# ConvFFN up-projection: the contraction in two halves of the rows, each half in banks of its own

## The chip, the cores and the metric

The kernel runs on one core of one Trainium2 chip. Its time is what the device took from start to end of one execution, in microseconds (us). Two executions of the kernel before took 2832.43 and 2834.16 us, median 2833.3. The core has five engines that run side by side, each through its own list of instructions in order: TensorE (PE; its weight loads stand apart as PEld), VectorE (DVE), ScalarE (ACT), GpSimd (POOL) and SyncE (SP, which starts the DMA transfers). An instruction that has to wait for another engine waits on a semaphore, and everything behind it on its own engine waits with it. TensorE multiplies a moving operand by a stationary one that a weight load has put in place; it sums over the 128 partitions (rows) of both and adds the result up in a bank of PSUM, of which there are eight.

## The reference

One step of a streaming encoder with four layers, over 512 prompt rows and 64 sample rows of width 1024. Each layer is a token mixer (attention, a convolution module or a spatial-gating MLP) followed by a channel mixer, and it is the latter that the change touches:

```python
def _conv_ffn(h, state, w_up, w_dw, b_dw, w_down):
    up = h @ w_up                                   # 1024 -> 2 * 2816
    xp = jnp.concatenate([state, up], axis=1)
    g, u = jnp.split(_dwconv(xp, w_dw, b_dw), 2, axis=-1)   # causal, width 3
    return (jax.nn.gelu(g) * u) @ w_down, xp[:, -(FFN_CONV_WIDTH - 1):]
```

RMSNorm stands before and after each mixer, and the results are added to the residual.

## The kernel before, in words

Activations lie transposed, channels on partitions and the 576 rows (512 and 64) along the free axis, which is cut into a half of 256 and a half of 320 columns. Every number is split into a high and a low part in fp32r, so that a product takes three matmuls for each 128 of the contraction: high by high, high by low, low by high (`mm3`, lines 278 to 280). With eight blocks of 128 in the width of 1024, a product of one half is 24 matmuls into one bank.

The channel mixer (`ffn`, called once a layer) runs over 22 pairs. Pair p holds 128 columns of the gate (q = 0) and the same 128 of the other branch (q = 1). `wload` fetches a weight tile, ScalarE casts its high part in two pieces of 512 columns (line 247) and VectorE takes the difference as the low part (line 250). Four buffers hold high parts, so the casts of pair p + 2 need the buffers of pair p. For each half (hf = 0 with 256 columns, hf = 1 with 320), `finish` runs product q = 0, then product q = 1, and then `evacuate`: VectorE multiplies a product by the norm's row factors and puts it from its bank into a buffer (`ub`, lines 791 and 793). After both halves come GpSimd's copies of the last columns (`fo`), then for each q a convolution of width 3 as one ScalarE activation (line 802) and two VectorE operations (803, 804), a GELU on ScalarE (806), the product of the two branches (808, 809), and the split of the result into `ah` (ScalarE cast, line 812) and `al` (VectorE, 813).

After pairs 3, 7, 11 and 15 a block of the down-projection runs (`block`, 192 matmuls into banks that VectorE adds to `o_y`, line 528), after pair 21 the last two. Pairs 0 and 1 of each layer are begun while the layer's first half ends (`between`), by an order written out by hand; all else is put in order by a scheduler at build time, which places every engine's instructions by a model of the durations, and the chip then follows that order.

Accumulators of all products share a pool of six banks (tag `mm`), two more banks serve small sums. A bank is taken when the first matmul of a product is written down (`bank`), and a later product that gets the same bank waits until the instructions that read it are done. The tag `t` of six work buffers holds the convolution's results.

The same halves of the rows, 0 to 63 and 64 to 127, are used by attention's scores (line 1108): 64 rows of contraction, one head in each half.

Of the kernel before, what the change touches and what calls it, by code (L numbers as in the profile page):

```python
# [12 lines left out]
ALU = mybir.AluOpType  # L13
# [4 lines left out]
P = 128  # L18
# [3 lines left out]
HALF = ((0, 256), (256, 320))  # L22
# [110 lines left out]
def encoder_step_kernel(  # L133
# [12 lines left out]
    V, S, G, T = nc.vector, nc.scalar, nc.gpsimd, nc.tensor  # L146
# [18 lines left out]
    def mm_tile(name):  # L165
        return mmp.tile([P, 512], F32, tag="mm", name=name)
# [13 lines left out]
    def w_tile(name, shape, dt=F32):  # L180
        return wp.tile(shape, dt, tag="t", name=name)
# [78 lines left out]
    def lo_eng(n):  # L260
        return V if n >= POOLW else None
# [10 lines left out]
    def mm3(ps, items, start=0, stop=None):  # L272
# [3 lines left out]
        for i in range(start, n if stop is None else stop):  # L276
# [2 lines left out]
            T.matmul(ps, lh, rl, start=False, stop=False)  # L279
            T.matmul(ps, ll, rh, start=False, stop=(i == n - 1))  # L280

    def bank(name, m=P, n=512):

        made = []

        def get():
            if not made:
                made.append(mm_tile(name)[:m, :n])
            return made[0]

        return get
# [24 lines left out]
    def finish(parts):  # L316
        for part in parts:
            if part:
                for product in part[0]:
                    product.all()  # L320
                part[1]()


    def rsqrt_steps(name, ps, n, scale, eps):
# [57 lines left out]
    def half(t, hf):  # L382
        a, n = HALF[hf]
        return t[:, a : a + n]
# [124 lines left out]
    class Output:  # L509
# [15 lines left out]
        def evacuate(self, m, hf, ps, first, last, square=True):  # L525
            ys = half(self.y[m], hf)
            if not first:
                V.tensor_tensor(ys, ps, ys, ALU.add)  # L528
            elif self.bias is not None:
                S.activation(ys, ps, AF.Identity, bias=self.bias[:, m : m + 1])  # L530
            else:
                S.copy(ys, ps)
            if last and square:
                self.sq[hf].add(ys)
                if self.final:
                    S.activation(ys, ys, AF.Copy, scale=gain(self.i, self.s, m))
# [221 lines left out]
    def ffn(i):  # L758
# [9 lines left out]
        def pair(p):  # L768
            n = f"f{i}_{p}"
            ws = []  # L770
            for q in range(2):
                ws.append(wload(f"{n}_w{q}", w_up, 0, KD, q * FF + p * P, P, lo_eng(p)))
                yield
            ub = []

            def begin():
                for q in range(2):
                    c = q * NF + p
                    ub.append(up.tile([P, 580], F32, tag="ub", name=f"{n}_ub{q}"))
                    G.memset(ub[q][:, 0:2], 0.0)  # L780
                    G.tensor_copy(ub[q][:, 514:516], ct[:, 4:6, c])

            for hf in range(2):
                ps = [bank(f"{n}_p{hf}{q}", n=HALF[hf][1]) for q in range(2)]

                def evacuate(hf=hf, ps=ps):
                    if hf == 0:
                        begin()
                    for q in range(2):
                        b = 2 + hf * 256  # L790
                        V.tensor_tensor(ub[q][:, b : b + 256], ps[q]()[:, :256], h.R[:, hf * 256 : hf * 256 + 256], ALU.mult)  # L791
                        if hf == 1:
                            V.tensor_tensor(ub[q][:, 516:580], ps[q]()[:, 256:320], h.R[:, 512:576], ALU.mult)

                yield [Product(ps[q], h.products(ws[q], hf)) for q in range(2)], evacuate
            cv = [None, None]
            for q in range(2):
                c = q * NF + p
                G.tensor_copy(fo[:, 0, :, c], ub[q][:, 512:514])  # L799
                G.tensor_copy(fo[:, 1, :, c], ub[q][:, 578:580])  # L800
                y = w_tile(f"{n}_c{q}", [P, 578])
                S.activation(y, ub[q][:, 2:580], AF.Identity, bias=ct[:, 3, c : c + 1], scale=ct[:, 2, c : c + 1])  # L802
                V.scalar_tensor_tensor(y, ub[q][:, 1:579], ct[:, 1, c : c + 1], y, ALU.mult, ALU.add)  # L803
                V.scalar_tensor_tensor(y, ub[q][:, 0:578], ct[:, 0, c : c + 1], y, ALU.mult, ALU.add)  # L804
                cv[q] = y
            S.activation(cv[0], cv[0], AF.Gelu_apprx_tanh)
            am = w_tile(f"{n}_a", [P, NT])
            V.tensor_tensor(am[:, 0:512], cv[0][:, 0:512], cv[1][:, 0:512], ALU.mult)
            V.tensor_tensor(am[:, 512:576], cv[0][:, 514:578], cv[1][:, 514:578], ALU.mult)  # L809
            a_hi[p] = b_tile(f"{n}_ah", [P, NT], F32R)  # L810
            a_lo[p] = b_tile(f"{n}_al", [P, NT], F32R)
            S.copy(a_hi[p], am)  # L812
            V.tensor_tensor(a_lo[p], am, a_hi[p].bitcast(F32), ALU.subtract)
# [13 lines left out]
        h = Norm(i, 2)  # L827
        begun = [pair(p) for p in range(2)]
        yield h, begun
        out = Output(i, 3)  # L830
        b = 0
        for p in range(NF):
            finish(begun[p] if p < 2 else pair(p))
            if b < len(FBLK) - 2 and p == sum(FBLK[b]) - 1 + FLAG:
                block(b)
                b += 1
# [1042 lines left out]
```

## Time and profile before

| | |
|---|---|
| median of two runs | 2833.3 us |
| profiled execution: time, span of its instructions | 2833.9 us, 2832.1 us |
| TensorE busy; its weight loads | 2758.0 us (97%); 2637.5 us (93%) |
| VectorE, ScalarE, GpSimd busy | 1857.0 us (66%), 1137.5 us (40%), 383.4 us (14%) |
| mean granted TensorE clock | 0.986 of full speed |
| up-projection matmuls (`f_p` on lines 278 to 280) | 8064, 13% of the chain on each line |
| down-projection matmuls (`o_p`, the same lines) | 9% of the chain on each line |

A busy share is an average over the whole span. Matmuls are pipelined: one lasts longer than the distance to the next, so the distance between starts tells the pace. The chain is followed back from the last instruction, at each step to what released it or to the instruction before it on its engine. An idle time in square brackets is that of the engine just before the instruction, with the one that ended it.

### The profile page before, as it was taken

The numbers are of one execution on the slowest core, as the hardware profiler recorded it, in microseconds if no ns is written. First come the engines' busy times: TensorE is split into PE (matmuls) and PEld (weight loads), VectorE is DVE, ScalarE is ACT, GpSimd is POOL, SyncE is SP. The second block draws the span as 40 slices with busy tenths as digits, with TensorE's granted clock in tenths as the row PEclk, the third lists the DMA queues.
The fourth block names the chain that finished last, engine by engine and source line by source line (L and its number), as shares of the span: only waits on it lengthen the run. The fifth ranks groups of instructions, "written<-read, shape, count | busy, mean of one in ns | idle before, by whom it ended". The sixth has DMA issues, their size and how long they took to land.

```text
span 2832.1 us, 52926 instructions
## 1 busy us (share of the span) xinstructions
PE 2758.0 (97%) x20841; PEld 2637.5 (93%) x20841; DVE 1857.0 (66%) x4194; ACT 1137.5 (40%) x2392; POOL 383.4 (14%) x937
## 2 busy tenths in 40 slices
PE   8999999999878999999999999999999999999998
PEld 7889999998666899999999999999999978999998
DVE  5668666656867576667657567666666676766674
ACT  4655433334123553334434324432333664533343
POOL 3122111110000021111002011211110121211111
PEclk9999999999888999999999999999999999999999
DMA  5322322322332232222233222322222421322221
GB/s 165 87 51 72 93 87 75 90 70 66 95 97 54 68 98 77 89 81 89 68 91 101 75 71 61 90 83 83 82 83 79 105 49 47 93 88 82 83 83 58
DMA packets 359183, 230.72 MB, mean 81 GB/s; under 512 B 44595, under 2 KB 349463, under 8 KB 358807
## 3 DMA queue, kind: packets, MB, share of 16 engines
q1 hardware_dynamic: 358934, 227.34, 28.0%
q8 instruction: 164, 2.69, 0.4%
q14 instruction: 85, 0.69, 0.1%
HBM read 212.87 MB, written 7.45 MB: 78 GB/s over the span
## 4 chain that ended last, share of the span: by engine, by line
PE 89%; DVE 4%; DMA 3%; SPq 2%; ACT 1%; issue 1%; POOL 0%; POOLq 0%; ACTq 0%; DVEq 0%
PE f_p L278 13%; PE f_p L279 13%; PE f_p L280 13%; PE o_p L278 9%; PE o_p L280 9%; PE o_p L279 9%; DVE v_cv L1380 2%; PE m_u_p L278 1%; PE m_u_p L280 1%; PE m_u_p L279 1%; PE m_vp L278 1%; PE m_vp L279 1%; PE m_vp L280 1%; PE t_o L1169 1%; PE t_qp L278 1%; PE t_sp L1108 1%
## 5 line engine op out<-in xcount | busy, mean ns | idle before, releaser
L278 PE MATMUL f_p<-n_hi,f_w_h 128*128 128x320 f32 (+1 forms) x2688 | 799.1, 297 | 0.0
L280 PE MATMUL f_p<-n_hi,f_w_l 128*128 128x320 f32 (+1 forms) x2688 | 797.3, 297 | 0.0
L279 PE MATMUL f_p<-n_lo,f_w_h 128*128 128x320 f32 (+1 forms) x2688 | 797.3, 297 | 0.0
L278 PEld LDWEIGHTS f_p<-n_hi,f_w_h 128*128 128x128 f32 x2688 | 510.1, 190 | 4.5 <-issue 4.1
L279 PEld LDWEIGHTS f_p<-n_lo,f_w_h 128*128 128x128 f32 x2688 | 510.1, 190 | 0.0
L280 PEld LDWEIGHTS f_p<-n_hi,f_w_l 128*128 128x128 f32 x2688 | 510.1, 190 | 0.0
L278 PE MATMUL o_p<-f_ah,f_d_h 128*128 128x256 f32 (+1 forms) x1408 | 418.8, 298 | 2.4 <-ACT f_d_h L247 2.4
L279 PE MATMUL o_p<-f_al,f_d_h 128*128 128x256 f32 (+1 forms) x1408 | 417.6, 297 | 0.0
L280 PE MATMUL o_p<-f_ah,f_d_l 128*128 128x256 f32 (+1 forms) x1408 | 417.2, 297 | 0.0
L247 ACT CAST f_w_h<-f_w_f 128x512 fp32r<-128x512 f32 x352 | 200.7, 618 | 494.9 <-issue 237.8
L528 DVE TENSOR_TENSOR o_y<-o_p,o_y 128x256 f32<-128x256 f32 (+1 forms) x432 | 195.1, 455 | 261.9 <-PE o_p L280 260.5
L791 DVE TENSOR_TENSOR f_ub<-f_p,n_R 128x256 f32<-128x256 f32 x352 | 148.1, 422 | 286.9 <-PE f_p L280 282.2
L278 PEld LDWEIGHTS o_p<-f_ah,f_d_h 128*128 128x128 f32 x1408 | 268.0, 190 | 4.2 <-ACT f_d_h L247 2.6
L280 PEld LDWEIGHTS o_p<-f_ah,f_d_l 128*128 128x128 f32 x1408 | 267.9, 190 | 0.4 <-issue 0.2
L279 PEld LDWEIGHTS o_p<-f_al,f_d_h 128*128 128x128 f32 x1408 | 268.0, 190 | 0.2 <-issue 0.2
L250 DVE TENSOR_TENSOR f_w_l<-f_w_f,f_w_h 128x512 fp32r<-128x512 f32 x352 | 228.9, 688 | 20.3 <-ACT f_w_h L247 18.2
L247 ACT CAST f_d_h<-f_d_f 128x512 fp32r<-128x512 f32 x176 | 101.3, 619 | 231.9 <-PE f_p L279 174.3
L803 DVE SCALAR_TENSOR_TENSOR f_c<-f_ub,f_ct,f_c 128x578 f32<-128x578 f32 x176 | 143.8, 820 | 38.2 <-ACT f_c L802 38.1
L799 POOL COPY f_fo<-f_ub 128x2 f32<-128x2 f32 x176 | 46.7, 266 | 888.0 <-DVE f_ub L791 881.1
L802 ACT ACTIVATE f_c<-f_ub,f_ct 128x578 f32<-128x578 f32 x176 | 150.8, 863 | 1.4 <-POOL f_fo L799 0.7
L812 ACT CAST f_ah<-f_a 128x576 fp32r<-128x576 f32 x88 | 59.2, 673 | 218.3 <-DVE f_a L809 218.3
L804 DVE SCALAR_TENSOR_TENSOR f_c<-f_ub,f_ct,f_c 128x578 f32<-128x578 f32 x176 | 143.3, 816 | 2.8
(374 smaller groups left out, 5637.5 us busy)
## 6 DMA issues: line engine op xcount, KB each, us to landing
f_w_f<-in_ffn_w_up_dram SPq DMA_DIRECT2D x176, 512.0 KB
f_d_f<-in_ffn_w_down_dram SPq DMA_DIRECT2D x80, 512.0 KB
v_w_f<-in_conv_w_pw_dram SPq DMA_DIRECT2D x24, 512.0 KB
v_g<-v_glu SPq DMA_DIRECT2D x128, 77.2 KB
t_wq_f<-in_attn_w_qkv_dram SPq DMA_DIRECT2D x32, 256.0 KB
t_wo_f<-in_attn_w_o_dram SPq DMA_DIRECT2D x32, 256.0 KB
m_wv_f<-in_cmlp_w_in_dram SPq DMA_DIRECT2D x16, 512.0 KB
m_u_w_f<-in_cmlp_w_in_dram SPq DMA_DIRECT2D x16, 512.0 KB
```

Of the source, the lines that this page charges most:

```text
L247: S.copy(hi[:, a:e], st[:, a:e])
L250: eng.tensor_tensor(lo[:, a:e], st[:, a:e], hi[:, a:e].bitcast(F32), ALU.subtract)
L278: T.matmul(ps, lh, rh, start=(i == 0), stop=False)
L279: T.matmul(ps, lh, rl, start=False, stop=False)
L280: T.matmul(ps, ll, rh, start=False, stop=(i == n - 1))
L528: V.tensor_tensor(ys, ps, ys, ALU.add)
L791: V.tensor_tensor(ub[q][:, b : b + 256], ps[q]()[:, :256], h.R[:, hf * 256 : hf * 256 + 256], ALU.mult)
L802: S.activation(y, ub[q][:, 2:580], AF.Identity, bias=ct[:, 3, c : c + 1], scale=ct[:, 2, c : c + 1])
L803: V.scalar_tensor_tensor(y, ub[q][:, 1:579], ct[:, 1, c : c + 1], y, ALU.mult, ALU.add)
L804: V.scalar_tensor_tensor(y, ub[q][:, 0:578], ct[:, 0, c : c + 1], y, ALU.mult, ALU.add)
L812: S.copy(a_hi[p], am)
L1380: V.scalar_tensor_tensor(self.cv, g, w, self.cv, ALU.mult, ALU.add)
```

## The change

In pairs 2 to 21 of every layer a full matmul over 128 rows becomes two, over rows 0 to 63 and rows 64 to 127 of the same operands. The first goes into the bank of its product (`p`), the second into a bank of its own (`r`). The two products of a half no longer follow each other: the code goes through the 24 steps and at each step writes q = 0 in both halves, then q = 1 in both (`mm3_halves`). The evacuation comes after both products: ScalarE copies bank `r` into a work buffer (line 813 of the changed file), VectorE adds bank `p` (814) and multiplies by the row factors (815, 817). Pairs 0 and 1 stay as they were. The matmuls of the changed pairs stand on line 291 of the changed file; its lines 830, 831, 832, 834, 836, 837, 840 and 841 are 802, 803, 804, 806, 808, 809, 812 and 813 of the file before.

```diff
--- before.py
+++ after.py
@@ -279,6 +279,17 @@
             T.matmul(ps, lh, rl, start=False, stop=False)
             T.matmul(ps, ll, rh, start=False, stop=(i == n - 1))
 
+    def mm3_halves(ps, items):
+
+
+        units = [[u for (lh, ll), (rh, rl) in its for u in ((lh, rh), (lh, rl), (ll, rh))] for its in items]
+        n = len(units[0])
+        for u in range(n):
+            for at in range(len(ps)):
+                l, r = units[at][u]
+                for q in range(2):
+                    T.matmul(ps[at][q](), l[64 * q : 64 * q + 64], r[64 * q : 64 * q + 64], start=(u == 0), stop=(u == n - 1))
+
     def bank(name, m=P, n=512):
 
         made = []
@@ -319,6 +330,13 @@
                 for product in part[0]:
                     product.all()
                 part[1]()
+
+
+    def finish_halves(parts):
+        for part in parts:
+            if part:
+                mm3_halves(part[2], [p.items for p in part[0]])
+                part[1](part[2])
 
 
     def rsqrt_steps(name, ps, n, scale, eps):
@@ -783,16 +801,26 @@
             for hf in range(2):
                 ps = [bank(f"{n}_p{hf}{q}", n=HALF[hf][1]) for q in range(2)]
 
-                def evacuate(hf=hf, ps=ps):
+                two = [[ps[q], bank(f"{n}_r{hf}{q}", n=HALF[hf][1])] for q in range(2)]
+
+                def evacuate(two=None, hf=hf, ps=ps):
                     if hf == 0:
                         begin()
                     for q in range(2):
                         b = 2 + hf * 256
+                        if two:
+                            t = w_tile(f"{n}_s{hf}{q}", [P, 320])[:, : HALF[hf][1]]
+                            S.copy(t, two[q][1]())
+                            V.tensor_tensor(t, ps[q](), t, ALU.add)
+                            V.tensor_tensor(ub[q][:, b : b + 256], t[:, :256], h.R[:, hf * 256 : hf * 256 + 256], ALU.mult)
+                            if hf == 1:
+                                V.tensor_tensor(ub[q][:, 516:580], t[:, 256:320], h.R[:, 512:576], ALU.mult)
+                            continue
                         V.tensor_tensor(ub[q][:, b : b + 256], ps[q]()[:, :256], h.R[:, hf * 256 : hf * 256 + 256], ALU.mult)
                         if hf == 1:
                             V.tensor_tensor(ub[q][:, 516:580], ps[q]()[:, 256:320], h.R[:, 512:576], ALU.mult)
 
-                yield [Product(ps[q], h.products(ws[q], hf)) for q in range(2)], evacuate
+                yield [Product(ps[q], h.products(ws[q], hf)) for q in range(2)], evacuate, two
             cv = [None, None]
             for q in range(2):
                 c = q * NF + p
@@ -830,7 +858,10 @@
         out = Output(i, 3)
         b = 0
         for p in range(NF):
-            finish(begun[p] if p < 2 else pair(p))
+            if p < 2:
+                finish(begun[p])
+            else:
+                finish_halves(pair(p))
             if b < len(FBLK) - 2 and p == sum(FBLK[b]) - 1 + FLAG:
                 block(b)
                 b += 1
```

The scheduler puts the new instructions in an order of its own. TensorE, layer 0, pair 10, where the second half's second product begins; a name such as `f0_10_p10` is layer 0, pair 10, bank p, half 1, product 0, and `_w0_h` is the high part of weight tile 0. Before:

```order
L279 MATMUL f0_10_p10_5099<-n0_2_lo6_2768,f0_10_w0_h_5027 128x320
L280 MATMUL f0_10_p10_5099<-n0_2_hi6_2760,f0_10_w0_l_5028 128x320
L278 MATMUL f0_10_p10_5099<-n0_2_hi7_2761,f0_10_w0_h_5027 128x320
L279 MATMUL f0_10_p10_5099<-n0_2_lo7_2769,f0_10_w0_h_5027 128x320
L280 MATMUL f0_10_p10_5099<-n0_2_hi7_2761,f0_10_w0_l_5028 128x320
L278 MATMUL f0_10_p11_5124<-n0_2_hi0_2754,f0_10_w1_h_5035 128x320 [waits DVE_49]
L279 MATMUL f0_10_p11_5124<-n0_2_lo0_2762,f0_10_w1_h_5035 128x320
L280 MATMUL f0_10_p11_5124<-n0_2_hi0_2754,f0_10_w1_l_5036 128x320
L278 MATMUL f0_10_p11_5124<-n0_2_hi1_2755,f0_10_w1_h_5035 128x320
```

After, from the 19th matmul of that half on:

```order
L291 MATMUL f0_10_p10_6051<-n0_2_hi3_2757,f0_10_w0_h_5923 128x320
L291 MATMUL f0_10_r10_6053<-n0_2_hi3_2757,f0_10_w0_h_5923 128x320
L291 MATMUL f0_10_p10_6051<-n0_2_lo3_2765,f0_10_w0_h_5923 128x320
L291 MATMUL f0_10_p11_6055<-n0_2_hi0_2754,f0_10_w1_h_5931 128x320 [waits Activation_49]
L291 MATMUL f0_10_p11_6055<-n0_2_lo0_2762,f0_10_w1_h_5931 128x320
L291 MATMUL f0_10_r11_6057<-n0_2_hi0_2754,f0_10_w1_h_5931 128x320 [waits Activation_49]
L291 MATMUL f0_10_r11_6057<-n0_2_lo0_2762,f0_10_w1_h_5931 128x320
L291 MATMUL f0_10_p11_6055<-n0_2_hi0_2754,f0_10_w1_l_5932 128x320
```

Before, product 1 begins when product 0 is complete, and waits for VectorE. Now 21 halves of product 0 stand ahead of it, two of each kind of product 1 stand side by side, and both banks of product 1 wait for ScalarE: `p11` for its copy `f0_10_s00`, `r11` for its copy `f0_10_s01`, which read the banks that they get. The same order stands in the 320-column half of 76 of the 80 changed pairs; in the 256-column half, 36 halves of product 0 stand ahead and three and three side by side in the pairs that do not follow a down-projection block or begin a layer.

ScalarE in the same place, from the casts of pair 11's weights to the next stage's evacuation. Before:

```order
L247 CAST f0_11_w0_h_5175<-f0_11_w0_f_5173 128x512 [waits DMAHW3_49,PE_49,Activation_49]
L247 CAST f0_11_w0_h_5175<-f0_11_w0_f_5173 128x512
L802 ACTIVATE f0_9_c0_5007<-f0_9_ub0_4943,f0_ct_2571 128x578 [waits DVE_49,Pool_49]
L247 CAST f0_11_w1_h_5183<-f0_11_w1_f_5181 128x512 [waits DMAHW4_49,PE_49,Activation_49]
L247 CAST f0_11_w1_h_5183<-f0_11_w1_f_5181 128x512
L806 ACTIVATE f0_9_c0_5007<-f0_9_c0_5007 128x578 [waits DVE_49]
L802 ACTIVATE f0_9_c1_5013<-f0_9_ub1_4946,f0_ct_2571 128x578 [waits DVE_49,Pool_49]
L812 CAST f0_9_ah_5021<-f0_9_a_5018 128x576 [waits DVE_49]
L247 CAST f0_d2_0_h_5323<-f0_d2_0_f_5321 128x512 [waits DMAHW5_49,PE_49,Activation_49]
L247 CAST f0_d2_0_h_5323<-f0_d2_0_f_5321 128x512
```

After (`s10` and `s11` are the copies of the 320-column half, `s00` and `s01` those of the 256-column half of the next pair):

```order
L247 CAST f0_11_w0_h_6183<-f0_11_w0_f_6181 128x512 [waits DMAHW3_49,PE_49,Activation_49]
L247 CAST f0_11_w0_h_6183<-f0_11_w0_f_6181 128x512
L247 CAST f0_11_w1_h_6191<-f0_11_w1_f_6189 128x512 [waits DMAHW4_49,PE_49,Activation_49]
L247 CAST f0_11_w1_h_6191<-f0_11_w1_f_6189 128x512
L813 COPY f0_9_s10_5891<-f0_9_r10_5793 128x320 [waits PE_49]
L813 COPY f0_9_s11_5896<-f0_9_r11_5797 128x320 [waits PE_49]
L830 ACTIVATE f0_9_c0_5903<-f0_9_ub0_5777,f0_ct_2571 128x578 [waits DVE_49,Activation_49,Pool_49]
L830 ACTIVATE f0_9_c1_5909<-f0_9_ub1_5780,f0_ct_2571 128x578 [waits DVE_49,Activation_49,Pool_49]
L834 ACTIVATE f0_9_c0_5903<-f0_9_c0_5903 128x578 [waits DVE_49]
L840 CAST f0_9_ah_5917<-f0_9_a_5914 128x576 [waits DVE_49]
L813 COPY f0_10_s00_6043<-f0_10_r00_5939 128x256 [waits PE_49]
L813 COPY f0_10_s01_6047<-f0_10_r01_5943 128x256 [waits PE_49]
```

Before, the casts of the two weight tiles stand apart, and nothing that TensorE waits for soon stands behind the convolution's activations. Now the four casts stand together ahead of the copies of pair 9's second half; their waits on TensorE are for the last matmuls of that half that use pair 9's high parts, of product 0 and of product 1. The copies of pair 10's first half, `s00` and `s01`, stand behind pair 9's convolution, GELU and cast of the result.

## Rows read from the trace of the kernel before

**Rows 1.** The page: its head, and the chain's shares by engine.
```profile
span 2832.1 us, 52926 instructions
...
PE 89%; DVE 4%; DMA 3%; SPq 2%; ACT 1%; issue 1%; POOL 0%; POOLq 0%; ACTq 0%; DVEq 0%
```

**Rows 2.** Groups by form: line, engine, operation, shapes, count | busy us, mean ns | idle.
```profile
L278 PE MATMUL f_p<-n_hi,f_w_h 128*128 128x320 f32 x1408 | 437.0, 310 | 0.0
L280 PE MATMUL f_p<-n_hi,f_w_l 128*128 128x256 f32 x1280 | 362.2, 283 | 0.0
L279 PEld LDWEIGHTS f_p<-n_lo,f_w_h 128*128 128x128 f32 x2688 | 510.1, 190 | 0.0
```

**Rows 3.** Timeline of TensorE in the up-projection: start us, duration us, instruction.
```profile
470.28 0.31 PE L279 MATMUL f_p<-n_lo,f_w_h 128*128 128x320 f32 x1
...
472.73 0.28 PE L278 MATMUL f_p<-n_hi,f_w_h 128*128 128x256 f32 x1
...
473.33 0.28 PE L280 MATMUL f_p<-n_hi,f_w_l 128*128 128x256 f32 x1
```

**Rows 4.** Timelines of matmuls and of weight loads around eight attention scores.
```profile
100.99 1.14 PE L1108 MATMUL t_sp<-t_k,t_q 64*128 64x256 f32 x8
102.05 0.38 PE L278 MATMUL t_qp<-n_hi,t_wq_h 128*128 128x256 f32 x1
...
101.31 0.41 PEld L1108 LDWEIGHTS t_sp<-t_k,t_q 64*128 64x128 f32 x4
```

**Rows 5.** Instructions of lines 1108 and 1389: duration ns min/median/max, first and last start.
```profile
L1108 PEld LDWEIGHTS t_sp<-t_k,t_q x256: 182/186/335, 63.9 to 2331.8; 64*128 64x128 f32 x128
L1108 PE MATMUL t_sp<-t_k,t_q x256: 272/376/789, 63.9 to 2332.0; 64*128 64x256 f32 x96, 64*128 64x128 f32 x32
...
L1389 PEld LDWEIGHTS v_pc<-v_g,v_dg x512: 106/110/178, 714.3 to 884.2; 128*32 128x32 f32 x171
```

**Rows 6.** Timeline of VectorE over one pair of the up-projection.
```profile
470.77 0.42 DVE L791 TENSOR_TENSOR f_ub<-f_p,n_R 128x256 f32<-128x256 f32 x1
471.11 0.21 DVE L793 TENSOR_TENSOR f_ub<-f_p,n_R 128x64 f32<-128x64 f32 x1
471.32 1.29 DVE L250 TENSOR_TENSOR f_w_l<-f_w_f,f_w_h 128x512 fp32r<-128x512 f32 x2
473.19 0.82 DVE L803 SCALAR_TENSOR_TENSOR f_c<-f_ub,f_ct,f_c 128x578 f32<-128x578 f32 x1 [0.58 <-ACT f_c L802]
...
475.11 0.69 DVE L808 TENSOR_TENSOR f_a<-f_c,f_c 128x512 f32<-128x512 f32 x1
```

**Rows 7.** Timeline of ScalarE over one pair of the up-projection.
```profile
467.15 1.15 ACT L247 CAST f_w_h<-f_w_f 128x512 fp32r<-128x512 f32 x2 [3.30 <-PE f_p L279]
...
470.67 1.14 ACT L247 CAST f_w_h<-f_w_f 128x512 fp32r<-128x512 f32 x2 [1.60 <-issue]
...
472.30 0.86 ACT L802 ACTIVATE f_c<-f_ub,f_ct 128x578 f32<-128x578 f32 x1
475.97 0.67 ACT L812 CAST f_ah<-f_a 128x576 fp32r<-128x576 f32 x1 [2.81 <-DVE f_a L809]
479.95 1.15 ACT L247 CAST f_d_h<-f_d_f 128x512 fp32r<-128x512 f32 x2 [3.30 <-PE f_p L279]
```

**Rows 8.** Groups by form of ScalarE and VectorE: reads of a bank.
```profile
L532 ACT COPY o_y<-o_p 128x320 f32<-128x320 f32 x32 | 13.6, 425 | 3.0 <-PE o_p L280 2.9
...
L528 DVE TENSOR_TENSOR o_y<-o_p,o_y 128x320 f32<-128x320 f32 x216 | 105.6, 490 | 185.5 <-PE o_p L280 184.3
```

**Rows 9.** Timeline of TensorE at two idle gaps (in square brackets).
```profile
78.43 0.82 PE L1108 MATMUL t_sp<-t_k,t_q 64*128 64x256 f32 x3 [1.38 <-DVE t_mx L1113]
...
811.13 0.39 PE L278 MATMUL v_p<-n_hi,v_w_h 128*128 128x256 f32 x1 [1.93 <-DVE v_t L1304]
```

**Rows 10.** Stretches behind these gaps: us; PE, PEld, DVE, ACT, POOL; clock; DMA, GB/s.
```profile
78.50:82.00 3.50, 3.50 (x24) 3.01 (x25) 3.36 (x18) 3.50 (x15) 0.77 (x2) 1.00 0.71 157
...
811.80:815.20 3.40, 3.14 (x14) 3.14 (x15) 3.40 (x8) 0.21 (x1) 0.00 (x0) 0.50 0.36 96
```

## The prediction

> **What bounds the kernel now.** I read the page's head and chain first, then the groups by form, then one pair of the up-projection in the timelines of each engine, then the places where other matmuls use half of the rows. TensorE holds 89% of the chain that ended last [rows 1], and the up-projection's matmuls show no idle time before them [rows 2]: VectorE and ScalarE work beneath it. Inside such a stretch a matmul of 256 columns starts 0.120 us after the one before it (five steps in 0.60 us) [rows 3]. The same cast recurs after 12.80 us, one pair later (467.15 to 479.95) [rows 7]; a pair has 48 matmuls of 256 and 48 of 320 columns, so one of 320 takes 12.80/48 - 0.120 = 0.147. I call 0.120 or 0.147 a slot. A matmul itself lasts 283 or 310 ns [rows 2], so neighbours overlap.
>
> **The change, part by part.** Two pairs of each of the four layers keep the old form. The other 80 pairs have 2 stages of 48 full matmuls, 7680 in all, that become 15360 half ones. The question is whether two halves share a slot.
>
> *Halves in one slot.* No half-row matmul of this type (fp32r) is in the trace. The nearest are the attention scores, 64 rows, fp32, alternating between rows 0-63 and 64-127. There 256 columns last 104 ns longer than 128 (376 against 272), so 256 stream for 0.21 us [rows 5]. Eight such matmuls one after another would last 7 by 0.21 + 0.38 = 1.85 us, two at a time 3 by 0.21 + 0.38 = 1.01; they took 1.14 [rows 4]. Two halves thus ran in the time of one, and four of their weight loads, 0.19 us each, went by in 0.41 us [rows 4, 5]. I take the same slot as before, 0.120 and 0.147, for two halves. Bounds: at best a slot loses all that exceeds the stream. Stream is (310-283)/64 = 0.42 ns a column [rows 2], so 0.107 and 0.134, and 0.013 us a slot may go; above, the same 0.013 may be paid once for each half: plus 0.013.
>
> *The order of the first matmuls.* A stage now uses four of the six banks and the next finds two free. In the usual order (14 of the 20 pairs) the first-product halves fill 18 slots of a 256 stage and 10 of a 320 stage; then the second product begins with halves of one kind side by side, three and three, or two and two, where the halves cannot share a slot: 3 and 2 slots lost.
>
> *The evacuation.* Its two ScalarE copies, two adds and two or four multiplications come after the whole stage, where before each product was evacuated on its own. The second product's banks are those of the copied halves, so TensorE waits for ScalarE's copies. What stands ahead of these on ScalarE decides. I walk through one usual pair, with time 0 where the 320 stage of the pair before ends its last slot. An independent instruction starts 0.08 us before its forerunner ends (0.42 us long, next one 0.34 later), one that needs another engine's result 0.03 to 0.08 after it (472.30 + 0.86 to 473.19) [rows 6, 7].
> - ScalarE: the casts of the weights two pairs on now wait for matmuls 4 slots before the end, since both products run to it: they start 0.39 us after such a matmul (470.28 to 470.67) [rows 3, 7], at -0.2. Four casts, two in 1.14 [rows 7], end near 2.0; the two copies of 0.43 [rows 8] end at 2.4 and 2.7.
> - TensorE: 18 slots to 2.16, waits to 2.4, six single halves (0.72), 27 slots: the 256 stage ends at 6.4, instead of 5.8.
> - VectorE: four weight differences (two in 1.29) to 3.0; adds of 0.49 each [rows 6, 8] to 3.8; multiplications of 0.42 and 0.21: the first product is whole at 4.3, the second at 4.8.
> - Then across ScalarE and VectorE: activations of 0.86 end at 5.2 and 6.0 [rows 7]; the four tap operations of 0.82, of which only the first waits, run 5.2 to 8.3; GELU is done by then; product 0.69 and its tail, and 0.86 us after its start the cast of the result, at 9.2 (475.11 to 475.97); it takes 0.67, to 9.9 [rows 6, 7].
> - Only now, behind that cast, come the copies of the 256 stage that ended at 6.4: done at 10.2 and 10.6.
> - TensorE's 320 stage starts at 6.4, has 10.5 slots of first-product work (to 8.0), then stands until 10.25. After that: four single halves in two waits (to 10.9) and 35.5 slots, 5.2 us: it ends at 16.1.
>
> So a usual pair takes 16.1 us where it took 12.8: 3.3 more, 2.2 of it in one wait. The chain does not shorten when TensorE is faster; it is a loop through stage end, casts, taps, copies, stage end.
>
> *The clock.* That wait is an idle gap of some 2.1 us (8.0 plus the last matmul's rest to 10.25). A gap of 1.93 us was followed by 3.4 us at a granted clock of 0.50, the lower level of 1.2 GHz; one of 1.38 us was not (1.00) [rows 9, 10]. 3.4 us at half speed do 1.7 us of work: 1.7 lost. Mine is nearest to the 1.93, but a single such case fixes no rule, so I charge half the pairs, 0.85 each, and keep 0 and 1.7 as bounds.
>
> *The sum.* 14 usual pairs in each of four layers, 56 by 3.3: 185 us. Pairs 2 and 3 have shorter queues (fewer casts ahead): I estimate 2.0 each, 8 by 2.0 = 16. Pairs 4, 8, 12 and 16 follow a down-projection block, which hides the chain; they lose only slots to single halves: 7 of 0.120 in pair 4, 2 of 0.147 in each, 2.0 a layer, 8. Changes between whole and half rows, some 40: the matmul after the eight scores started at 102.05, where the last two had started at about 101.75 (1.14 us of the eight less 0.38), so some 0.09 later than one slot of theirs; 4 us [rows 4]. Together 213, and the clock 56 by 0.85 = 48: 261 us. From the span of 2832.1 [rows 1] that gives 3093, with the 1.8 us around it 3095; the profiled run of 2833.9 stands 0.6 above the median of 2833.3, which I neglect. The time of the added copies, adds and multiplications is in the walk; the rest of it lies beside matmuls (ScalarE idled 2.81 us before that cast, and 3.30 before others [rows 7]).
>
> **Rivals.**
> (A) *Halves one after another.* Each full matmul becomes two slots: 3840 by (0.120 + 0.147) = 1025 us more. The stages last over 11 us and hide the chain; with 12 us for the singles and changes, 3870. Against it: the eight scores in 1.14 us [rows 4].
> (B) *Weight loads one after another.* A load of 128 columns takes 186 ns, one of 32 columns 110 [rows 5], so 0.79 ns a column and 0.10 us for 128, beside a fixed part. If the two loads of a slot could not overlap, a slot would be 0.20 us; a stage 9.7, a pair some 20.2 with its singles, and the chain nearly hidden: 80 by 7.4 = 590, so 3430. Against it: four such loads took 0.41 us [rows 4], where 3 by 0.10 + 0.19 = 0.49 would be the least one after another. The Trainium skill ("TensorE: Matmul & The Clock Gate", LDWEIGHTS) says that a load's time goes by its columns and not by its rows, so that halving rows saves none of it. By that rule, the trace agrees: 186 ns for 64 rows [rows 5], 190 for 128 [rows 2].
> (C) *Faster.* If a half's weights load wholly behind the other rows' matmul and the slot falls to its stream, 7680 by 0.013 = 100 us go, 2734, provided that the wait on the copies stays away. That would need the copy of the 256 stage to end before 8.0 instead of 10.2, so that the taps and activations ahead of it shrink by 2.2 of their 10 us; no row speaks for that. With the wait, the gain counts only for the 40 slots behind it, 0.5 us a pair. The Trainium skill ("TensorE: Matmul & The Clock Gate", Packing small matmuls) states that weight loads overlap running matmuls only where the rows differ, by which this change would hide loads that were bare before; the trace differs, since loads of 190 ns stood in slots of 120 on the same rows [rows 2, 3].
> (D) *No difference.* The halves share slots and the chain runs ahead of its walk, say because ScalarE's copy is reached by 8.5: then 0.6 us a pair remain, 56 by 0.6 plus 28, less the slot gain of up to 100: within 2% of before, near 2835.
>
> **How the numbers follow.** Forecast 3095: chance 0.81, with its inner bounds. Rival A 0.05, B 0.05, C 0.04, D 0.05. The forecast's low end: no low clock (-48), slots 0.013 shorter on the 40 slots behind the wait (-0.5 by 56 = -28), a chain 0.6 us shorter (-34): 2985. Its high end: low clock in every usual pair (+48), slots 0.013 longer (+28 and +15 in the other pairs), a chain 0.5 us longer (+28): 3215. The range 2985 to 3215 leaves out A to D, 0.19 together. Faster by over 2% (about what a measurement of this kernel can tell from none) is C, 0.04; within 2% is D, 0.05; slower is the rest, 0.91.
>
> **What would show it.** Halves in pairs of starts a few ns apart, with 0.120 and 0.147 between pairs: slots right; 0.24 and more: A; 0.20: B. An idle row of TensorE before the second product of nearly each 320 stage, some 2.1 us, released by the ScalarE copy: the chain is right; none: wrong, and C or D likely. ScalarE's copies starting right behind the result's cast, 3 us after their stage ended: the queue is right. Granted clock under 1.00 in many up-projection slices: the gap costs clock too. TensorE's idle time of a pair well under 2 us with a longer total would mean that the slots grew.

## The result, and the profile after

The changed kernel takes 3111.0 us (median of 3107.64 and 3114.29), 1.098 times the time before, with a 95% interval of 1.0962 to 1.0997: 9.8% slower. The forecast was 3095 (2985 to 3215). The profiled execution has a span of 3112.5 us, 280.4 more than the 2832.1 before [rows 1].

First the mean granted TensorE clock of the whole run, before and after:

```profile
core 0: 2832.1 us, clock 0.986
```

```profile
core 0: 3112.5 us, clock 0.967
```

The page of after, its costliest matmul group (columns as in [rows 2]):

```profile
L291 PE MATMUL f_p<-n_hi,f_w_h 64*128 64x256 f32 (+1 forms) x2560 | 695.5, 308 | 146.9 <-ACT f_s L813 145.4
```

Before, the up-projection had no idle time ahead of its matmuls [rows 2]. Now 146.9 us stand ahead of the first product steps of bank `p`, 145.4 of them ended by ScalarE's copies. Timeline of TensorE where a 320 stage ends and a 256 stage begins:

```profile
493.78 0.31 PE L291 MATMUL f_p<-n_hi,f_w_l 64*128 64x320 f32 x1
493.79 0.31 PE L291 MATMUL f_r<-n_hi,f_w_l 64*128 64x320 f32 x1
493.93 0.31 PE L291 MATMUL f_p<-n_hi,f_w_l 64*128 64x320 f32 x1
...
494.08 0.28 PE L291 MATMUL f_p<-n_hi,f_w_h 64*128 64x256 f32 x1
494.09 0.28 PE L291 MATMUL f_r<-n_hi,f_w_h 64*128 64x256 f32 x1
494.19 0.28 PE L291 MATMUL f_p<-n_lo,f_w_h 64*128 64x256 f32 x1
...
494.55 0.28 PE L291 MATMUL f_p<-n_lo,f_w_h 64*128 64x256 f32 x1
```

The two halves start 0.01 us apart, and the next two 0.15 later (320 columns), or 0.12 (494.08 to 494.55 is four steps in 0.47): the slots of before [rows 3], now with two halves in each. Where the halves alternate, the slots are as long as before; the loss lies where TensorE stands. The same timeline one usual pair later, and ScalarE's over that pair:

```profile
504.31 0.41 PE L291 MATMUL f_p<-n_hi,f_w_h 64*128 64x320 f32 x1 [2.22 <-ACT f_s L813]
...
520.50 0.61 PE L291 MATMUL f_p<-n_hi,f_w_h 64*128 64x320 f32 x1 [2.25 <-ACT f_s L813]
```

```profile
510.05 2.18 ACT L247 CAST f_w_h<-f_w_f 128x512 fp32r<-128x512 f32 x4 [5.53 <-issue]
512.14 0.74 ACT L813 COPY f_s<-f_r 128x320 f32<-128x320 f32 x2
514.59 1.63 ACT L830 ACTIVATE f_c<-f_ub,f_ct 128x578 f32<-128x578 f32 x2 [1.70 <-DVE f_ub L817]
517.84 0.69 ACT L834 ACTIVATE f_c<-f_c 128x578 f32<-128x578 f32 x1 [1.62 <-DVE f_c L832]
519.50 0.67 ACT L840 CAST f_ah<-f_a 128x576 fp32r<-128x576 f32 x1 [0.98 <-DVE f_a L837]
520.08 0.64 ACT L813 COPY f_s<-f_r 128x256 f32<-128x256 f32 x2
```

Casts, copies of the 320 stage, convolution, GELU, cast of the result, and only then the copies of the 256 stage, whose last matmul had started at 516.50. The first of them, some 0.35 us long, ends at about 520.43, and TensorE goes on at 520.50. In the whole trace 56 such gaps of 2.22 to 2.26 us stand in the 320 stages. Windows over two usual pairs and over the stretch behind the second gap (us; PE, PEld, DVE, ACT, POOL; clock; DMA, GB/s):

```profile
504.31:520.50 16.19, 13.90 (x192) 13.43 (x193) 10.20 (x22) 6.36 (x13) 2.28 (x8) 1.00 0.22 66
520.50:538.08 17.58, 15.34 (x192) 14.87 (x192) 10.20 (x22) 6.36 (x13) 2.27 (x8) 0.90 0.20 62
520.70:524.00 3.30, 3.30 (x25) 3.30 (x27) 1.60 (x5) 0.02 (x1) 0.00 (x0) 0.51 0.02 5
```

A pair takes 16.19 us, and 17.58 where a stretch at the lower clock (1.2 GHz) follows the gap; the gap at 504.31 was followed by none. 32 of the 56 were.

### The profile page after: what moved, and what is told of

The parts are those of the page before. It is cut to its first block, busy times and chain, and to the rows that moved or that the text cites. A ratio compares the mean times of both kernels' runs of the same rounds, so it can differ in the third digit from the quotient of the medians.

```text
span 3112.5 us, 68798 instructions
## 1 busy us (share of the span) xinstructions
PE 2890.0 (93%) x28521; PEld 2732.1 (88%) x28521; DVE 1944.3 (62%) x4514; ACT 1241.1 (40%) x2712; POOL 352.2 (11%) x937
## 5 line engine op out<-in xcount | busy, mean ns | idle before, releaser
L291 PE MATMUL f_p<-n_hi,f_w_h 64*128 64x256 f32 (+1 forms) x2560 | 695.5, 308 | 146.9 <-ACT f_s L813 145.4
L291 PE MATMUL f_r<-n_hi,f_w_h 64*128 64x256 f32 (+1 forms) x2560 | 692.9, 308 | 0.2 <-DVE f_s L814 0.2
L291 PE MATMUL f_p<-n_lo,f_w_h 64*128 64x256 f32 (+1 forms) x2560 | 678.7, 302 | 0.0
L291 PE MATMUL f_r<-n_lo,f_w_h 64*128 64x256 f32 (+1 forms) x2560 | 667.2, 302 | 0.0
L291 PE MATMUL f_p<-n_hi,f_w_l 64*128 64x256 f32 (+1 forms) x2560 | 666.4, 302 | 0.0
L291 PE MATMUL f_r<-n_hi,f_w_l 64*128 64x256 f32 (+1 forms) x2560 | 663.4, 301 | 0.0
L291 PEld LDWEIGHTS f_p<-n_hi,f_w_h 64*128 64x128 f32 x2560 | 465.4, 194 | 179.1 <-ACT f_s L813 175.2
L291 PEld LDWEIGHTS f_r<-n_lo,f_w_h 64*128 64x128 f32 x2560 | 465.2, 195 | 0.2 <-issue 0.2
L291 PEld LDWEIGHTS f_r<-n_hi,f_w_h 64*128 64x128 f32 x2560 | 464.3, 193 | 0.4 <-DVE f_s L814 0.4
L291 PEld LDWEIGHTS f_p<-n_lo,f_w_h 64*128 64x128 f32 x2560 | 464.5, 193 | 0.0
```

Of the source, the lines that this page charges most:

```text
L291: T.matmul(ps[at][q](), l[64 * q : 64 * q + 64], r[64 * q : 64 * q + 64], start=(u == 0), stop=(u == n - 1))
```

## Experiments

Theory W is that of the prediction: halves share a slot, and the loss is the wait on copies queued behind the convolution, with the clock behind it. Rival H: the half-row matmuls themselves cost. Rival V: the added copies and additions are too much for ScalarE and VectorE. Each ratio is to runs of the kernel before that were taken along with it (medians 2831.5 to 2833.3 us).

| run | time, us | of before (95% interval) | mean clock |
|---|---|---|---|
| changed kernel | 3111.0 | 1.098 (1.0962 to 1.0997) | 0.967 |
| per_product | 2860.8 | 1.0103 (1.0088 to 1.0118) | 0.985 |
| per_product4 | 2838.0 | 1.0022 (1.0013 to 1.0031) | 0.989 |
| full_rows | 2849.1 | 1.0059 (1.0044 to 1.0074) | 0.986 |
| full_rows4 | 2830.3 | 0.9994 (0.9985 to 1.0003) | 0.989 |
| early_copy | 2904.4 | 1.0259 (1.0242 to 1.0277) | 0.984 |
| mid_copy | 2964.6 | 1.0467 (1.0437 to 1.0498) | 0.985 |
| one_tap | 2979.5 | 1.052 (1.049 to 1.0551) | 0.985 |
| longer | 3181.9 | 1.1235 (1.1194 to 1.1276) | 0.959 |
| full_late | 3065.6 | 1.0824 (1.0793 to 1.0856) | 0.963 |
| serial | 3600.7 (one run) | | 0.989 |

### The halves kept, the place of the evacuation changed: per_product

```diff
-                mm3_halves(part[2], [p.items for p in part[0]])
-                part[1](part[2])
+                for q in range(2):
+                    mm3_halves(part[2][q : q + 1], [part[0][q].items])
+                    part[1](part[2], qs=(q,))
```

(`evacuate` then goes through `qs` alone.) The two products of a half follow each other again, so this run changes their order and the place of the evacuation together.

> All half-row matmuls, all ScalarE copies and all additions stay; only their place changes: the two halves of one product alternate, its bank pair is evacuated as soon as that product ends, and then comes the next product, as in the kernel before. A product's banks are now wanted again three products later, over 9 us after its end. Theory W (the loss is the wait of the second product's first halves on copies that stand behind the convolution on ScalarE, with the clock drop behind it): no idle row of TensorE before a product, pair 12.8 us, granted clock as in the kernel before, 2837 us (2833 and some 4 for the changes between whole and half rows). Rival H (the half-row matmuls themselves cost, in slots or in clock): they are all still here, so near 3110. Rival V (the added copies and additions load ScalarE and VectorE too much): they are all still here, so near 3110 too.

Measured 2860.8, so H and V fall: every half, copy and addition is still there, and 250 of the 278 us are gone. A usual pair, in the windows of this run:

```profile
464.67:477.47 12.80, 12.80 (x197) 12.80 (x194) 10.56 (x21) 6.35 (x12) 2.09 (x8) 1.00 0.30 85
```

12.80 us and a full clock as before, with 197 matmuls recorded in it instead of some 98, and VectorE busy for 10.56 of them. But 24 us more were left than expected. They are not in the pairs. Windows of layer 0 of this run, from the first up-projection matmul to the first down-projection block, and from there to the fifth; and the same two of the kernel before:

```profile
214.96:283.50 68.54, 66.03 (x678) 61.38 (x677) 55.13 (x137) 35.65 (x74) 12.90 (x34) 0.98 0.19 56
283.50:605.93 322.43, 322.43 (x4129) 320.88 (x4128) 230.18 (x457) 137.78 (x264) 34.48 (x140) 1.00 0.29 86
```

```profile
214.88:278.57 63.69, 63.69 (x486) 59.79 (x485) 53.04 (x132) 34.26 (x67) 17.47 (x34) 1.00 0.19 56
278.57:598.57 320.00, 320.00 (x2402) 320.00 (x2401) 204.21 (x386) 113.86 (x191) 42.15 (x140) 1.00 0.29 86
```

4.9 us are lost at the start of the layer (18.0 in all four), 2.4 between the blocks (10 in all). Some 1.5 of these 2.4 stand where whole and half rows take turns:

```profile
348.57 0.31 PE L291 MATMUL f_r<-n_hi,f_w_l 64*128 64x320 f32 x1
348.81 0.39 PE L278 MATMUL o_p<-f_ah,f_d_h 128*128 128x256 f32 x1
349.03 0.28 PE L279 MATMUL o_p<-f_al,f_d_h 128*128 128x256 f32 x1
```

Two steps of 0.24 and 0.22 us stand here in place of 0.147 and 0.120, so a change costs 0.19 us. The other 0.9 lies in the four pairs behind the first block; its cause is open.

### The same from pair 4 on: per_product4, full_rows4

```diff
+            elif p < 4:
+                finish((part or ())[:2] for part in pair(p))
```

> The run per_product (half-row matmuls, copies and additions, each product evacuated by itself; 1.010 of before), but from pair 4 of each layer on, so that pairs 2 and 3 keep the old form. In per_product's trace 18.0 of its extra us stand between the start of a layer's up-projection and its first down-projection block (2.6 to 6.6 a layer, waits for ScalarE copies that stand behind the convolutions of pairs 0 and 1), and 2.5 a layer between later blocks. Theory W: the first part goes, the rest stays: 10 us over before, ratio 1.0035 (1.002 to 1.005). If half-row matmuls cost something in every pair, as rival H has it, 72 pairs would show it here: 1.007 or more.

> The run full_rows (whole rows, two banks, copies and additions; 1.006 of before) from pair 4 of each layer on. In full_rows' trace all of the extra 17.5 us stand at the starts of the layers, 0.0 between the later blocks. Theory W: no difference from before, ratio 1.000 (0.999 to 1.0015). The distance to per_product4, some 9 us, is then what half-row matmuls cost with no wait about: the changes between whole and half rows.

Both as forecast, but per_product4 costs 1.0022 rather than 1.0035, at the low end of what was given. The starts of the layers were the rest, and with pairs 2 and 3 in the old form two banks with their copies and additions cost nothing that can be measured (full_rows4, 0.9985 to 1.0003). Half rows (per_product4) cost 6 us more than the kernel before, 0.2%, and 7.7 more than full_rows4 (9 had been expected), and gain nothing. Its trace has 32 changes between blocks and half rows; by the 0.19 us above they make 6.1 us.

### Two banks, whole rows: full_rows

```diff
-                for q in range(2):
-                    T.matmul(ps[at][q](), l[64 * q : 64 * q + 64], r[64 * q : 64 * q + 64], start=(u == 0), stop=(u == n - 1))
+                T.matmul(ps[at][u % 2](), l, r, start=(u < 2), stop=(u >= n - 2))
```

> Two banks for each product, ScalarE copy, addition and evacuation after both products as in the changed kernel, but whole-row matmuls: the 24 steps of a product go by turns to its two banks. No half-row matmul. The scheduler, whose durations fit these matmuls, puts the copies of the 256-column half ahead of the cast of the result, behind GELU, and the copied banks are wanted only after 24 slots of a 320 stage (3.5 us). Theory W: the copy is at 8.1 us of the pair, wanted at 9.3: no wait, 2840 us (2830 to 2860). Rival V: the evacuation is as heavy as in the changed kernel, so above 3000. Rival H: near 2835 as well, since no halves are left; this run tells V from the other two.

Measured 2849.1: V falls a second time. From the first to the fifth block of layer 0 the window has exactly the time of before:

```profile
285.03:605.03 320.00, 320.00 (x2403) 320.00 (x2401) 224.59 (x458) 140.52 (x265) 43.33 (x140) 1.00 0.29 86
```

All of its 17.5 us stand at the starts of the layers, and 12.5 of them are waits for the same copies.

### Only ScalarE's order: early_copy, mid_copy

The tail of a pair (convolution to cast) is written down behind the next pair's first evacuation, and ScalarE is held to that order; `mid_copy` writes the part up to GELU ahead of it and the cast behind it. In this excerpt of early_copy, `prev` is what is still to be written of the pair before.

```diff
...
-                mm3_halves(part[2], [p.items for p in part[0]])
-                part[1](part[2])
+        for first in (True, False):
+            part = next(u for u in parts if u)
+            mm3_halves(part[2], [p.items for p in part[0]])
+            with tc.manual_schedule(engines={mybir.EngineType.Activation}):
+                part[1](part[2])
+                if first:
+                    for _ in prev:
+                        pass
...
```

> TensorE's order, halves and banks as in the changed kernel; only ScalarE's order differs: the two copies of the 256-column half stand ahead of the convolution, GELU and cast of the pair before, where they stood behind them. Theory W: the copies end 0.4 to 0.7 us after their stage, before TensorE wants the bank 1.5 us after it, so the wait of 2.25 us in each usual 320 stage goes, and with it the clock drops; the pair is 13.7 us (12.8 and the 0.9 of single halves and of the short wait in the 256 stage) instead of 16.2; 56 pairs by 0.9 and some 25 for the other pairs: 2910 us (2895 to 2930). Rival H or V: no change, near 3110. If only the wait goes and the clock still drops, about 2960.

Measured 2904.4. ScalarE of this run behind a 256 stage: the copies now start as their stage ends, and the convolution follows them. Below it the window of one usual pair:

```profile
489.95 0.65 ACT L819 COPY f_s<-f_r 128x256 f32<-128x256 f32 x2 [3.82 <-PE f_r L291]
490.48 1.64 ACT L836 ACTIVATE f_c<-f_ub,f_ct 128x578 f32<-128x578 f32 x2
```

```profile
483.46:496.82 13.36, 13.36 (x196) 13.16 (x194) 10.15 (x22) 6.35 (x13) 2.27 (x8) 1.00 0.24 80
```

All gaps of the usual pairs are gone, the mean clock is back at 0.984, and the pair is 13.36 us. With the same TensorE order in these pairs, the queue on ScalarE was thus worth 2.8 of the 3.4 us of each pair, and the clock besides; VectorE's convolution moved with it, so that the order of both engines is tested, not that of one.

> The changed kernel with one thing moved: on ScalarE the copies of the 256-column half stand between GELU and the cast of the result of the pair before, no longer behind the cast. TensorE's order is that of the changed kernel. There the GELU of a usual pair ends at 518.53, the copies start at 520.08. Theory W (the pair is a loop through stage end, casts, convolution, copies, and each microsecond that the copies come earlier comes off it): the copy 1.55 us earlier, the wait 0.70 instead of 2.25, the pair 14.65 instead of 16.2; and no low clock behind so short a gap. 55 pairs by 1.55 = 85, and the clock's 27 by 1.4 = 38, less: 2985 us (2960 to 3010). If the clock drops come from the half-row matmuls and not from the gap, they stay, and it is 3025.

Measured 2964.6. The gap, in the timeline of TensorE, is shorter still than forecast (the first copy starts 0.1 us before GELU ends, which the forecast had left out), and its 56 repetitions were followed by a low clock not once:

```profile
483.96 0.41 PE L291 MATMUL f_p<-n_hi,f_w_h 64*128 64x320 f32 x1 [0.57 <-ACT f_s L821]
```

### The chain shorter and longer: one_tap, longer

```diff
-                V.scalar_tensor_tensor(y, ub[q][:, 0:578], ct[:, 0, c : c + 1], y, ALU.mult, ALU.add)
+                if p < 2:
+                    V.scalar_tensor_tensor(y, ub[q][:, 0:578], ct[:, 0, c : c + 1], y, ALU.mult, ALU.add)
```

```diff
+            if p >= 2:
+                S.copy(am, am)
             S.copy(a_hi[p], am)
```

> The changed kernel without the third tap of the convolution in the changed pairs (this part of the computation is left out): two VectorE operations of 0.82 us less in the chain, in which the second two of four overlap nothing. ScalarE's queue, TensorE's order, halves and banks stay. Theory W: GELU starts as soon as the second activation is done, the product 1.5 us earlier, so the copies too: wait 0.75, pair 14.7, no clock drops: 2990 us (2965 to 3015). A rival that puts the wait on the copies themselves or on TensorE's own order expects no change of the wait: near 3100.

> The changed kernel with one ScalarE copy more (the product of the branches onto itself, 128x576, about 0.67 us, 0.08 of it beside its neighbour) ahead of the cast of the result; the outputs stay the same. Theory W: the copies behind it come 0.6 us later, the wait is 2.85, the undisturbed pair 16.8. The clock drop should follow more of the gaps than the 27 of 55 in the changed kernel. 55 by 0.6 = 33 and some 8 drops more by 1.4: 3155 us (3135 to 3180). If the wait were set elsewhere, near 3111.

Measured 2979.5 and 3181.9 (2 us above what was given). The gaps, first in one_tap, then in longer:

```profile
486.71 0.41 PE L291 MATMUL f_p<-n_hi,f_w_h 64*128 64x320 f32 x1 [0.77 <-ACT f_s L813]
```

```profile
513.26 0.41 PE L291 MATMUL f_p<-n_hi,f_w_h 64*128 64x320 f32 x1 [2.93 <-ACT f_s L813]
```

1.5 us less of VectorE's work took 1.5 off the gap, 0.6 more of ScalarE's put 0.7 on it. The chain sets the pair, microsecond by microsecond (14.66 us in one_tap, 14.46 in mid_copy, 16.19 in the changed kernel). None of the 55 gaps of 0.8 us in one_tap was followed by a low clock, and 38 of the 53 of 2.9 us in longer were. (For the changed kernel the forecast of longer counted 27 of 55; over its whole trace it is 32 of 56.)

### The wait with whole rows: full_late

```diff
...
+            with tc.manual_schedule(engines={mybir.EngineType.Activation}):
+                if first:
+                    for _ in prev:
+                        pass
+                part[1](part[2])
...
+                for _ in range(4):
+                    S.copy(am, am)
             S.copy(a_hi[p], am)
```

(on full_rows)

> Whole-row matmuls with two banks for each product (the run full_rows, 2849 us, which had no wait in its usual pairs), but ScalarE's copies of the 256-column half stand behind the convolution, GELU and cast of the pair before, and four copies of the branches' product onto itself (0.67 us each) stand ahead of that cast. In full_rows that cast ends 8.5 us after the pair began; 2.5 more make 11.0, the copy ends at 11.4, and TensorE wants its bank at 9.3. So: a wait of some 2.1 us in each usual 320 stage with not one half-row matmul. Theory W: the wait costs the same here, pair 15.0, and a low clock follows about half of the gaps: 2849 + 56 by 2.2 + 28 by 1.4 = 3010 us (2975 to 3045). If the drops belong to half-row matmuls: no low clock, 2972.

Measured 3065.6, 20 over the range. The forecast took one wait of 2.1 for all pairs; they came out as 1.66, some 2.1 and 3.55, since the scheduler did not give all pairs the same order. But the clock is answered. Two gaps in the timeline, and the windows behind them (us; PE; clock; DMA, GB/s):

```profile
427.66 0.41 PE L290 MATMUL f_r<-n_lo,f_w_h 128*128 128x320 f32 x1 [1.66 <-ACT f_s L818]
...
442.92 0.42 PE L290 MATMUL f_r<-n_lo,f_w_h 128*128 128x320 f32 x1 [2.20 <-ACT f_s L818]
```

```profile
443.10:446.50 3.40, 3.40 (x15) 0.54 0.02 5
427.80:431.20 3.40, 3.40 (x24) 1.00 0.00 0
```

Behind the gap of 2.20 the clock is at 0.54 on average, behind the one of 1.66 at 1.00. With no half row in these stages, a low clock follows the gaps of 1.77 to 2.21 us (all 26), 11 of the 15 of some 3.55, and none of the 16 of 1.65 to 1.68. So it needs no half-row matmul and belongs to the gap, but not by the gap's length alone.

### Halves that don't alternate: serial

```diff
-        for u in range(n):
-            for at in range(len(ps)):
+        for at in range(len(ps)):
+            for q in range(2):
+                for u in range(n):
```

> The same half-row matmuls, but those of one kind stand together: 24 on rows 0-63, then 24 on rows 64-127, then the next product. All pay a slot of their own, as the single halves side by side did (0.120 and 0.147 us in the changed kernel's trace). 3840 by 0.267 = 1025 us more than before, and stages of 11.5 and 14 us hide the copies: 3860 us (3820 to 3900). If halves did not share a slot at all in the changed kernel, it would be the same as that kernel; if the chip reorders them, near 2840.

Measured 3600.7: much slower, so alternation is what lets halves share, but 260 us better than forecast. The timeline where 24 matmuls on rows 64 to 127 (`f_r`) end and, in the order of the program, 24 on rows 0 to 63 (`f_p`) begin:

```profile
502.80 0.28 PE L291 MATMUL f_r<-n_hi,f_w_l 64*128 64x256 f32 x1
502.81 0.41 PE L291 MATMUL f_p<-n_hi,f_w_h 64*128 64x320 f32 x1
502.92 0.28 PE L291 MATMUL f_r<-n_hi,f_w_h 64*128 64x256 f32 x1
503.04 0.28 PE L291 MATMUL f_r<-n_lo,f_w_h 64*128 64x256 f32 x1
503.06 0.31 PE L291 MATMUL f_p<-n_lo,f_w_h 64*128 64x320 f32 x1
503.16 0.28 PE L291 MATMUL f_r<-n_hi,f_w_l 64*128 64x256 f32 x1
503.21 0.31 PE L291 MATMUL f_p<-n_hi,f_w_l 64*128 64x320 f32 x1
```

The first three of the new run start beside the last three of the old. 80 pairs have 8 runs each, 640 in all; if three slots of 0.134 are saved at each, as here, that is 256 us, and 3858 (2833 and the 1025 of the forecast) less 256 is 3602.

## Why the prediction was right, point by point

The forecast lay 16 us under the measurement, and its steps can be set beside the trace. The mechanism was right; two terms, the starts of the layers and the changes of rows, were sized too small.

- **Slots.** Two halves in one slot of 0.120 and 0.147: right, in the changed kernel and in per_product. Rivals A and B, serial halves or serial weight loads, are out (B's terms add up to 3423, not 3430, which changes nothing here). The gain of up to 0.013 us a slot did not come: per_product's pair is 12.80. The Trainium skill ("TensorE: Matmul & The Clock Gate", Packing small matmuls) says that weight loads overlap running matmuls only where the rows differ; the trace of the kernel before decides otherwise, since loads of 190 ns on the same rows lay under its matmuls [rows 2, 3], so no bare load was left to hide. What the remaining 0.013 us of a slot is was not measured.
- **The walk through a pair.** With the pair's start at 494.08 for TensorE's gap, and one pair later at 510.27 (16.19 on) for ScalarE's rows: casts at -0.2, first activation at 4.3, cast of the result at 9.2, TensorE going on at 10.2 (504.31). The walk came to the same places within 0.1 us, and its pair of 16.1 is 16.19.
- **The single halves** cost less than the 0.9 us (with the short wait) that the walk gave them: early_copy's pair is 13.36, 0.56 over 12.80. The timelines of serial and of the changed kernel (last section) show a way: the next halves on the other rows start beside them. The pair is set by the loop through ScalarE, so the difference lengthened the gap (2.22 to 2.26 us where the walk had 2.1) and did not show in the sum.
- **The clock.** Half of the gaps were charged 1.7 us each, 48 in all; 32 of 56 paid 1.4 (17.58 less 16.19), 45. The choice between "none" and "all" was a guess that came out; the gap of 1.93 us in [rows 9] happened to be a good neighbour.
- **Pairs 2 and 3** were one term that was mis-sized. It was put at 16 us on the ground that their queues are shorter. Windows of layer 0 of the changed kernel, cut as those of before above:

```profile
215.20:288.82 73.62, 67.46 (x678) 62.65 (x676) 53.21 (x133) 35.12 (x72) 12.04 (x32) 0.95 0.16 49
288.82:668.02 379.20, 347.52 (x4130) 339.43 (x4129) 222.50 (x456) 136.63 (x263) 37.42 (x140) 0.97 0.25 74
```

The start of the layer has 9.9 us more than before, and 33 in all four layers. ScalarE there:

```profile
258.34 1.14 ACT L247 CAST f_w_h<-f_w_f 128x512 fp32r<-128x512 f32 x2 [1.68 <-DMA f_w_f<-in_ffn_w_up_dram]
259.50 1.28 ACT L834 ACT_TABLE_LOAD   x1
260.80 0.69 ACT L834 ACTIVATE f_c<-f_c 128x578 f32<-128x578 f32 x1
261.39 1.61 ACT L830 ACTIVATE f_c<-f_ub,f_ct 128x578 f32<-128x578 f32 x2
...
265.29 0.69 ACT L834 ACTIVATE f_c<-f_c 128x578 f32<-128x578 f32 x1 [1.73 <-DVE f_c L832]
265.88 0.62 ACT L813 COPY f_s<-f_r 128x256 f32<-128x256 f32 x2
```

Pair 2's first copies stand behind the convolutions of both pairs 0 and 1, a cast that waited for its weights' transfer, and the load of a table for GELU: the queue is longer there, not shorter. Waits for the same copies are 10.4 of per_product's 18.0 us there, and 12.5 of full_rows' 17.5.

- **Changes of rows** were the other: 0.09 us each, from the matmul behind the scores, where per_product shows 0.19, and the changed kernel the same two steps of 0.24 and 0.22 at each. Forty of them are 8 us, not 4. In the sum this is hidden, since the pairs behind a block, put at 8 us, came to less.
- **The sum.** Usual pairs 56 by 3.39 = 190 (185 forecast), their clock 45 (48), the starts of the layers 33 (16), all else between the first down-projection block of a layer and its last two about 8 (12, for the other pairs and the changes of rows), everything else 4 (0): 280 us, where the forecast had 261. The last 4 stand in the last two down-projection blocks of layer 0: there TensorE waits 2.0 us for a transfer that the next mixer needs, a wait that the kernel before does not have, and the lower clock lasts 10.2 us instead of 3.4. The forecast had no term for that place.

Rivals C and D needed the copies before TensorE wants their bank. early_copy made them so, by another order, and even then the halves ran 2.6% behind before, not ahead: C's slot gain does not exist here, and per_product4, without these waits, is not faster either (1.0022).

Why the scheduler put the copies behind the convolution was not tried. That the same scheduler, given whole rows, put them ahead of the cast (full_rows) fits a model that takes two halves for two slots and so sees no hurry; this is argued, not shown. Open too is why a gap of 2.25 us lowers the clock in 32 of 56 cases, when in full_late all 21 between 2.07 and 2.21 did, and only 11 of 15 of some 3.55.

## What to carry to other kernels

Before splitting an accumulation over more banks, follow each bank's release to the engine that frees it and read what stands ahead of that instruction in its queue: here 207 of 278 us went when two copies of 0.35 us stood earlier in ScalarE's queue (early_copy), and 250 when the order of the products changed as well (per_product), with the twice as many matmuls still there. A queue's order is safe only for the slack that it was made with, so an evacuation that TensorE will wait for belongs ahead of work that nobody waits for. And price half-row matmuls by the trace of the same kernel: here the weight loads already lay beneath whole-row matmuls, and halves shared a slot and gave back nothing.

## What had not been expected of the hardware

Matmuls on other rows overtake. In serial the first three matmuls of a run on rows 0 to 63 started up to three slots ahead of older ones on rows 64 to 127 (502.81 beside 502.80, while 502.92 to 503.16 were still to start). The Trainium skill ("TensorE: Matmul & The Clock Gate", Step-by-step: what each phase is for) states that only weight loads are pulled ahead and matmuls stay in program order; this run shows otherwise for matmuls on different rows, and the 256 us saved agree with it. The changed kernel shows the same on a small scale. Behind the gap at 504.31 its order is two `f_p`, two `f_r`, `f_p`, as in the order listing above, but the third `f_p` starts ahead of the second `f_r`:

```profile
504.58 0.41 PE L291 MATMUL f_r<-n_hi,f_w_h 64*128 64x320 f32 x1
504.71 0.30 PE L291 MATMUL f_p<-n_hi,f_w_l 64*128 64x320 f32 x1
504.83 0.30 PE L291 MATMUL f_r<-n_lo,f_w_h 64*128 64x320 f32 x1
```

A gap of about 2.2 us on TensorE can cost 3.6: 2.2 for itself and 1.4 for the 3.3 us at half clock (0.51) that may follow. Gaps up to 0.8 us (111 in mid_copy and one_tap) and of 1.65 to 1.68 us (16 in full_late) were free of that.
